# First five feature tiles of a hybrid trunk: half of the tokens projected without its shift, the shift's own projection added at evacuation

## The chip, the cores and the metric

The kernel runs on one core of a Trainium2 chip. The metric is the device time of one execution in microseconds (us); several executions of the kernel before took 1582.78 to 1583.99 us, median 1583.34. Engines are PE (TensorE, the matmuls; its weight loads are listed as PEld), DVE (VectorE), ACT (ScalarE), POOL (GpSimd) and SP, whose queue issues the transfers from device memory (DRAM) to the on-chip memory SBUF. Matmul results go to PSUM, eight banks of 2 KB for each of 128 partitions.

## The reference, cut to what matters

One inference step of a two-layer trunk over 640 tokens (128 context tokens and 512 latent ones) of 1024 features. Layer 0 runs a Conformer convolution and a bidirectional mLSTM side by side on one input projection:

```
mod = silu(cond) @ w_mod[l] + b_mod[l]             # cond: one vector for context, one for latent tokens
shift, scale, gate, ... = split(mod, 6)
h = x * rsqrt(mean(x*x, features) + eps) * g * (1 + scale) + shift
p = h @ w_in_ab
ga, gg, q, k, v, o, gates = split(p)
u = ga * sigmoid(gg)                               # then 31 taps along the tokens, layer norm, silu
gates = gates + b_gate                             # log-space scans over the tokens, once forward, once backward
```

Shift, scale and gate are one row of 1024 features for all context tokens and one for all latent tokens. Where the text below says A, it means g * (1 + scale), times the normalised x; h @ W is then the projection of the scaled x plus the projection of the shift. Layer 1 is attention; each layer is followed by a SwiGLU network. Everything is float32.

## The kernel before

The activations lie with the features on the partitions: xT is [128 partitions, 8 feature blocks k, 640 tokens]. The tokens are worked on in two halves of 320 (`HF`); in the first half the first 128 tokens are context and have their own column of the modulation (`RANGES`). Float32 accuracy comes from splitting both operands into a high and a low part and issuing three matmuls for each block k (`mm3`, L185 to L190): weight-high by H-high (L188), weight-high by H-low (L189), weight-low by H-high (L190). A feature tile for one half is 8 x 3 = 24 matmuls of 320 columns. ACT makes a high part (a copy to the rounded type), DVE or POOL the low part (source minus high part): of weights in `split_w` (L105, L108), at the start in halves (`split_half`, L586, L588), of activations in `split_to` (L464, L465).

**The first five feature tiles** of layer 0 are two tiles of convolution u0 (gg and ga), the tile of the gates, and two tiles of convolution u1. `start_norm` (L550) prepares what they need, and `proj_A(start=True)` (L413) runs them: first half of the tokens, blocks 0 to 3 of all five tiles, blocks 4 to 7 of all five tiles, then the second half tile by tile. Between the tiles it calls pieces of `start_norm` that were put into `pending` (`third`, `fourth`, `tail`, `late`). `start_norm` does, for a half:

- squares of x on ACT (L610, L613), added on DVE (L614);
- `rstd_T` (L382): sum over the partitions by two matmuls with a matrix of ones (L387, listed as four passes), root on ACT (L388) with a load of its table, reciprocal on DVE (L389), all 128x320;
- scaling of x by it, two of four tiles on DVE and two on POOL (L622).

The modulation of the whole norm comes in four pieces (which, half): which is 0 for the shift and 1 for the scale, half is features 0 to 511 or 512 to 1023. A piece takes eight row matmuls (`mod_rows`, L243), a transpose on DVE (`rows_T`, L259), four small matmuls (L250) and an add (L253, in `mod_cols`). For the first half, x is multiplied by A (L634, L636), and the shift is added as H is written (L641 on ACT for the high part, L642 on DVE for the low part), so PE's first projection matmul stands behind the pieces (1,0) and (0,0). For the second half, `modulate` (L400, L402) and `split_to` write H.

**Loads** go through SP's queue, in program order: x of the first half, eight of the modulation (L569), halves of the five weight tiles (L577) with the rest of the modulation between them, x of the second half, the other weight halves. Later modulation rows (layer 0's other pieces, blocks of 128x512) come through `mfill` (L193) and a ring of seven buffers, `mraw`; later weights through two `raw` buffers (L93).

**What comes after**: the evacuations of the conv tiles (sigmoid on ACT, L737, product on DVE, L740), of the gates (L1030, `gate_evac`); a copy of gate rows between partitions by DMA (L1089); `gate_rows` (L818): log-sigmoid on ACT (L830 to L832), scans on DVE that give M (L849, L857, L859), its split; projection of v (`v_in`), whose PSUM tiles are emptied by ACT (L1060); eight feature tiles (u2, q and k, u3, ...); a block of small matmuls on the gates (L887, L894) that ACT's copies, exponentials (L878, L900) and evacuations (L1069) release; further feature tiles. Beside all that DVE, ACT and POOL work on the 31 taps of the convolutions in the background: 21 on DVE (L756, L758), ten products on ACT (L762, L766) which POOL adds up (L767).

PSUM: tag `p1` has six buffers here, `cy` one of two banks. A scheduler fixes the order of the instructions on each engine from the program and its own model of durations; engines wait for each other by semaphores.

## Time and profile before

| | |
|---|---|
| time, median of 3 runs (lowest, highest) | 1583.34 us (1582.78, 1583.99) |
| the profiled execution: its own time | 1582.84 us |
| the profiled execution: span of the core | 1580.9 us |
| PE busy | 1520.2 us, 96% |
| DVE busy | 947.8 us, 60% |
| ACT busy | 583.7 us, 37% |
| POOL busy | 589.2 us, 37% |
| mean granted clock of PE over the span | 0.985 |

The span runs from the first to the last instruction of the profiled execution; all times below count from its start. A row of the trace with xcount over 1 stands for instructions of the same form that follow one another. What an instruction waited for stands in brackets. Busy time overlaps between engines; the chain of waits says which of it sets the end.

### The profile page before, as it was taken

The numbers are of one execution on the slowest core, as the hardware profiler recorded it, in microseconds if no ns is written. First come the engines' busy times: TensorE is split into PE (matmuls) and PEld (weight loads), VectorE is DVE, ScalarE is ACT, GpSimd is POOL, SyncE is SP. The second block draws the span as 40 slices with busy tenths as digits, with TensorE's granted clock in tenths as the row PEclk, the third lists the DMA queues.
The fourth block names the chain that finished last, engine by engine and source line by source line (L and its number), as shares of the span: only waits on it lengthen the run. The fifth ranks groups of instructions, "written<-read, shape, count | busy, mean of one in ns | idle before, by whom it ended". The sixth has DMA issues, their size and how long they took to land.

```text
span 1580.9 us, 23994 instructions
## 1 busy us (share of the span) xinstructions
PE 1520.2 (96%) x9597; PEld 1404.1 (89%) x9597; DVE 947.8 (60%) x1484; ACT 583.7 (37%) x1166; POOL 589.2 (37%) x386
## 2 busy tenths in 40 slices
PE   6898999999999999999998999999999999999998
PEld 4788988879999999999997777899998998999996
DVE  4788842647994785646768588847763423333335
ACT  3556547525222221213134437644531221212223
POOL 1479611215322112313133445524424534434241
PEclk8999999999999999999999999999999999999999
DMA  9223132442453342314352220022320321312221
GB/s 367 102 71 134 44 107 88 136 161 94 153 180 115 115 152 94 134 60 148 107 172 108 81 80 16 26 107 82 121 91 35 107 80 54 107 54 81 80 67 67
DMA packets 63684, 165.13 MB, mean 104 GB/s; under 512 B 6951, under 2 KB 13999, under 8 KB 63573
## 3 DMA queue, kind: packets, MB, share of 16 engines
q1 hardware_dynamic: 63572, 163.60, 30.1%
q8 instruction: 75, 1.23, 0.3%
q14 instruction: 37, 0.30, 0.1%
HBM read 157.45 MB, written 6.03 MB: 103 GB/s over the span
## 4 chain that ended last, share of the span: by engine, by line
PE 76%; DVE 13%; issue 4%; ACT 3%; POOL 1%; DMA 1%; SPq 0%; ACTq 0%; DVEq 0%; POOLq 0%
PE p L188 23%; PE p L189 23%; PE p L190 23%; DVE acc L220 2%; DVE t L400 1%; DVE H L465 1%; PE p L243 1%; PE p L1333 1%; DVE t L389 1%; ACT w L105 1%; DVE cy L758 1%; PE p L1353 1%; POOL t L767 1%; DVE w L108 1%; DVE acc L218 0%
## 5 line engine op out<-in xcount | busy, mean ns | idle before, releaser
L188 PE MATMUL p<-H,w 128*128 128x320 f32 x1968 | 611.5, 313 | 4.5 <-ACT h L900 1.2
L189 PE MATMUL p<-H,w 128*128 128x320 f32 x1968 | 610.8, 311 | 5.2 <-DVE H L465 5.2
L190 PE MATMUL p<-H,w 128*128 128x320 f32 x1968 | 607.7, 310 | 0.1
L108 POOL TENSOR_TENSOR w<-raw,w 128x1024 fp32r<-128x1024 f32 x124 | 316.6, 2557 | 682.2 <-ACT w L105 655.2
L188 PEld LDWEIGHTS p<-H,w 128*128 128x128 f32 x1968 | 370.4, 189 | 13.4 <-issue 3.9
L189 PEld LDWEIGHTS p<-H,w 128*128 128x128 f32 x1968 | 371.7, 189 | 11.8 <-DVE H L465 6.4
L190 PEld LDWEIGHTS p<-H,w 128*128 128x128 f32 x1968 | 370.8, 189 | 1.0 <-DVE w L588 0.5
L105 ACT ACTIVATE w<-raw 128x1024 fp32r<-128x1024 f32 x180 | 188.5, 1056 | 378.0 <-PE p L190 252.9
L220 DVE SCALAR_TENSOR_TENSOR acc<-mraw,cs,acc 128x512 f32<-128x512 f32 x196 | 175.9, 944 | 0.0
L1437 DVE TENSOR_TENSOR t<-t,p 128x320 f32<-128x320 f32 x88 | 42.6, 484 | 205.7 <-ACT t L1436 137.8
L478 DVE SCALAR_TENSOR_TENSOR h<-p,modT,h 128x128 f32<-128x128 f32 (+2 forms) x189 | 74.4, 430 | 67.6 <-PE p L190 67.5
L465 DVE TENSOR_TENSOR h<-t,h 128x320 fp32r<-128x320 f32 x88 | 93.5, 1063 | 33.0 <-ACT h L464 33.0
L188 PE MATMUL p<-h,w 128*128 128x320 f32 x352 | 108.7, 309 | 2.2 <-DVE t L1437 1.5
L1436 ACT ACTIVATE t<-p 128x320 f32<-128x320 f32 x88 | 38.3, 436 | 195.3 <-PE p L190 195.3
L189 PE MATMUL p<-h,w 128*128 128x320 f32 x352 | 108.7, 309 | 0.0
L190 PE MATMUL p<-h,w 128*128 128x320 f32 x352 | 108.3, 308 | 0.0
L108 DVE TENSOR_TENSOR w<-raw,w 128x1024 fp32r<-128x1024 f32 x56 | 77.5, 1384 | 42.4 <-ACT w L105 42.4
L471 DVE TENSOR_TENSOR t<-p,h 128x512 f32<-128x512 f32 (+1 forms) x61 | 41.4, 681 | 82.8 <-PE p L190 82.7
L472 POOL TENSOR_TENSOR h<-h,t 128x512 f32<-128x512 f32 x50 | 69.2, 1387 | 51.5 <-DVE t L471 51.4
L189 PE MATMUL p<-w,h 128*128 128x512 f32 (+1 forms) x224 | 87.5, 390 | 0.0
L190 PE MATMUL p<-w,h 128*128 128x512 f32 (+1 forms) x224 | 87.3, 390 | 0.0
L188 PE MATMUL p<-w,h 128*128 128x512 f32 (+1 forms) x224 | 87.0, 388 | 0.0
(315 smaller groups left out, 2228.0 us busy)
## 6 DMA issues: line engine op xcount, KB each, us to landing
raw<-in_wfi SPq DMA_DIRECT2D x88, 512.0 KB, 3.6
mraw<-in_wmod SPq DMA_DIRECT2D x160, 256.0 KB, 3.0
raw<-in_wfo SPq DMA_DIRECT2D x44, 512.0 KB, 3.5
raw<-in_wab SPq DMA_DIRECT2D x16, 512.0 KB, 3.5
raw<-in_wc SPq DMA_DIRECT2D x12, 512.0 KB, 3.5
h<-in_xT SPq DMA_DIRECT2D x16, 320.0 KB, 5.6
wm<-in_wmod SPq DMA_DIRECT2D x8, 512.0 KB, 7.8
h<-in_wmod SPq DMA_DIRECT2D x8, 512.0 KB, 8.2
```

What stands on the lines that cost most here:

```text
L105: self.nc.scalar.activation(hi, r, AF.Copy)
L108: e.tensor_tensor(lo, r, hi.bitcast(F32), ALU.subtract)
L188: t.matmul(out, w[0], x[0], start=first, stop=False)
L189: t.matmul(out, w[0], x[1], start=False, stop=False)
L190: t.matmul(out, w[1], x[0], start=False, stop=last)
L220: nc.vector.scalar_tensor_tensor(acc[:, c], w, s, bias if k == 0 else acc[:, c], ALU.mult, ALU.add)
L465: j = self.nc.vector.tensor_tensor(lo, src, hi.bitcast(F32), ALU.subtract)
L471: nc.vector.tensor_tensor(tmp, ps, gate, ALU.mult)
L472: (e or nc.gpsimd).tensor_tensor(x, x, tmp, ALU.add)
L478: self.nc.vector.scalar_tensor_tensor(x, ps[:, b - a * HF:e - a * HF], gate[:, k, c:c + 1], x, ALU.mult, ALU.add)
L1436: nc.scalar.activation(s[:, sl], pg, AF.Silu)
L1437: nc.vector.tensor_tensor(s[:, sl], s[:, sl], pu, ALU.mult)
```

## The change

It concerns the first five feature tiles only.

1. **First half without shift.** `no_shift` (in place of `times_A` and `plus_shift`) writes the first half's H as x*A: high part on ACT, low part on DVE by one instruction that multiplies and subtracts. The second half's H has the shift as before.
2. **The shift's projection.** H has 32 more columns; two of them take the split shift of the context and latent tokens. The second half's matmuls run over 322 columns instead of 320, so the last two columns of each tile's result are the shift's own projection. ACT copies them to SBUF (five small copies), and they are added as a bias when the first half's PSUM tile is emptied: in the sigmoid, in the product, in the gates' bias. The first half of a tile is therefore evacuated only after its second half was projected, and the tiles' order in the second half is u1, u0, gates.
3. **`rstd_P`** in place of `rstd_T` at the start: sums over the partitions by six one-column matmuls with the tokens on the partitions, root and reciprocal of 128x3 instead of 128x320, spreading by three matmuls into PSUM; scaling is all on DVE and reads that PSUM tile. The load of ACT's table is issued before it (`self.table()`).
4. **Order.** The scale pieces (1,0) and (1,1) come first, the shift pieces (0,0) and (0,1) after the first half's projection (`fifth`), the second of them through eight `mraw` buffers' turns. Loads follow: scale rows and weight halves, then x of the second half, then the shift rows. `mraw` has six buffers instead of seven. H of the first half with its shift, which v and all later tiles read, is written by `last`, under the second half's projection.
5. `start_proj` holds this loop; `proj_A` loses its `start` branch.

The diff, cut to its core (L-numbers of the printed code above are of before):

```diff
-        while self.mq and len(self.mready) < 7:
+        while self.mq and len(self.mready) < 6:
...
+        self.Hall = c.tile([P, KD, 2, TOK + 32], FR, name="H")
+        self.Hbuf = self.Hall[:, :, :, :TOK]
...
+        def dma_k(which, half):
+            for k in range(KD):
+                r = wm[which, half, k] = mraw()
+                nc.sync.dma_start(r, I["wmod"][0, 2 * which + half, k // 2][:, (k % 2) * 512:(k % 2 + 1) * 512])
...
-        def scale(a, on_pool):
-            r = self.rstd_T([sums[a][:, 0], sums[a][:, 1]], sums[a][:, 0])
+        def scale(a):
+            r = self.rstd_P([sums[a][:, 0], sums[a][:, 1]])
             sl = slice(a * HF, (a + 1) * HF)
             for i in range(4):
-                e = nc.gpsimd if i in on_pool else nc.vector
-                e.tensor_tensor(xT[i][:, :, sl], xT[i][:, :, sl], r.unsqueeze(1).to_broadcast([P, 2, HF]), ALU.mult)
+                nc.vector.tensor_tensor(xT[i][:, :, sl], xT[i][:, :, sl], r.unsqueeze(1).to_broadcast([P, 2, HF]),
+                                        ALU.mult)
...
+        def no_shift(k):
             for b, e, c in RANGES[0]:
...
+                w, A, hi = xT[k // 2][:, k % 2, b:e], m[:, 1, k, c:c + 1], H[:, k, 0, b:e]
+                nc.scalar.activation(hi, w, AF.Copy, scale=A)
+                nc.vector.scalar_tensor_tensor(H[:, k, 1, b:e], w, A, hi.bitcast(F32), ALU.mult, ALU.subtract)
         for i in range(4):
+            self.load_x(i, 0, xT[i])
+        dma(1, 0)
         for i in range(2):
             dma_w(i, 0, mraw())
+        dma(1, 1)
         for i in range(2, 5):
             dma_w(i, 0, mraw())
         rw = [self.pool.tile([P, 1024], F32, tag="raw", name="raw", bufs=2) for _ in range(2)]
         for i in range(5):
             dma_w(i, 1, rw[i // 2][:, (i % 2) * 512:(i % 2 + 1) * 512] if i < 4 else mraw())
+        for i in range(4):
+            self.load_x(i, 1, xT[i])
+        dma(0, 0)
...
+        self.table()
+        scale(0)
         mm((1, 0))
         cols(1, 0)
...
+            no_shift(k)
...
+        def second():
             mm((1, 1))
             for i in range(2, 5):
                 split_half(i, 0)
             cols(1, 1)
             for k in range(4, 8):
+                no_shift(k)
+        def third():
+            for i in range(5):
+                split_half(i, 1)
+            dma_k(0, 1)
+            for i in range(4):
+                squares(1, i)
         def fourth():
+            self.table()
+            scale(1)
+        def fifth():
+            mm((0, 0))
+            cols(0, 0)
+            mm((0, 1))
             cols(0, 1)
             for i in range(4):
                 to_H(1, i)
+            sh = m[:, 0]
+            hi, lo = (self.Hall[:, :, j, TOK:TOK + 2] for j in range(2))
+            self.split_to(hi, lo, sh)
+        def last():
+            for i in range(4):
+                to_H(0, i)
+        self.pending += [second, third, fourth, fifth, last]
...
+    def rstd_P(self, sums):
+        nc = self.nc
+        pt = self.p1()
+        blocks = ((0, 0), (P, 0), (HF - P, 2 * P - (HF - P)))
+        for j, (b, _) in enumerate(blocks):
+            for i, ss in enumerate(sums):
+                nc.tensor.matmul(pt[:, j:j + 1], ss[:, b:b + P], self.one8[:, 0:1], start=(i == 0),
+                                 stop=(i == len(sums) - 1))
+        r = self.col(8)
+        self.root = nc.scalar.activation(r[:, 0:3], pt[:, 0:3], AF.Sqrt, bias=self.eps, scale=1.0 / D).ins,
+        nc.vector.reciprocal(r[:, 4:7], r[:, 0:3])
+        pr = self.p1()[:, :HF]
+        for j, (b, o) in enumerate(blocks):
+            nc.tensor.matmul(pr[:, b + o:b + P], r[:, 4 + j:5 + j].to_broadcast([P, P]), self.ident[:, o:], start=True,
+                             stop=True)
+        return pr
+
+    def start_proj(self, H, jobs, bg):
...
+        tiles = [(i, j) for i, job in enumerate(jobs) for j in range(len(job[0]))]
+        for n, (i, j) in enumerate(tiles):
+            mm(i, j, 0, range(4))
+            self.pend((1, 4).count(n))
+        for n, (i, j) in enumerate(tiles):
+            mm(i, j, 0, range(4, KD))
+            self.pend((2, 4).count(n))
+        for n, i in enumerate((2, 0, 1)):
+            ws, evac = jobs[i]
+            for j in range(len(ws)):
+                mm(i, j, 1, range(KD))
+            if n == 0:
+                self.pend(1)
+            bias = []
+            for j in range(len(ws)):
+                b = self.col(2)
+                nc.scalar.activation(b, outs[i, j, 1][:, HF:], AF.Copy)
+                bias.append(b)
+            evac(slice(0, HF), *[outs[i, j, 0] for j in range(len(ws))], bias=bias)
+            evac(slice(HF, TOK), *[outs[i, j, 1][:, :HF] for j in range(len(ws))])
+            self.tick(bg[0] / 6, bg[1] / 6)
+            self.wdone(len(ws))
```

The order of the instructions on three queues, before and with the change (line numbers of each kernel's own code; `p` and `cy` are PSUM tiles, `H` the activations, `w` weights, `wm`, `h` and `mraw` buffers of modulation rows, `cs` the conditioning vectors, `fsel` a selection matrix, `xcount` at the end as in the profile).

PE, from its start to the first projection matmul; before:

```order
L669 MATMUL p_147<-ident 128x128 x18
L387 MATMUL p_176<-t,one_76 128x320 x2
L243 MATMUL p_185<-wm,cs 32x512 x8
L250 MATMUL p_196<-t,fsel 32x8 x4
L243 MATMUL p_211<-wm,cs 32x512 x8
L250 MATMUL p_231<-t,fsel 32x8 x4
L669 MATMUL p_237<-ident,t 128x128 x4
L188 MATMUL p_272<-H,w 128x320
```

and with the change:

```order
L650 MATMUL p_141<-ident 128x128 x18
L711 MATMUL p_172<-one_76,t 128x1 x6
L718 MATMUL p_182<-ident,col 128x128 x2
L718 MATMUL p_182<-ident,col 128x64
L243 MATMUL p_190<-wm,cs 32x512 x8
L250 MATMUL p_201<-t,fsel 32x8 x4
L188 MATMUL p_247<-H,w 128x320
```

One modulation piece (L243, L250) instead of two stands ahead of the first projection matmul, and the norm's matmuls have one column in place of 320.

PE, where the first half's projection ends (in `cy`) and the second half's begins; before:

```order
L190 MATMUL cy<-H,w 128x320
L188 MATMUL p_515<-H,w 128x320
L188 MATMUL p_540<-H,w 128x320
L188 MATMUL p_583<-H,w 128x320
L188 MATMUL p_614<-H,w 128x320
L188 MATMUL p_639<-H,w 128x320
L189 MATMUL p_515<-H,w 128x320
```

and with the change:

```order
L190 MATMUL cy<-H,w 128x320
L243 MATMUL p_467<-h,cs 32x512 x8
L250 MATMUL p_478<-t,fsel 32x8 x4
L243 MATMUL p_484<-mraw,cs 32x512 x8
L250 MATMUL p_495<-t,fsel 32x8 x4
L188 MATMUL p_519<-H,w 128x322
L188 MATMUL p_544<-H,w 128x322
L188 MATMUL p_619<-H,w 128x322
L189 MATMUL p_519<-H,w 128x322
```

Both shift pieces, sixteen row matmuls and eight small ones, have moved from ahead of the first half and from within it to this place.

SP's queue around the copy of the gate rows (`h<-h`); before:

```order
L197 DMA mraw<-in_wmod 128x512 x5
L93 DMA raw<-in_wv 128x1024 x2
L197 DMA mraw<-in_wmod 128x512
L93 DMA raw<-in_wv 128x1024 x2
L93 DMA raw<-in_wab 128x1024
L1089 DMA h<-h 36x640
L197 DMA mraw<-in_wmod 128x512 x4
L93 DMA raw<-in_wab 128x1024 x3
```

and with the change:

```order
L93 DMA raw<-in_wv 128x1024 x2
L566 DMA mraw<-in_wmod 128x512
L93 DMA raw<-in_wv 128x1024
L566 DMA mraw<-in_wmod 128x512 x2
L197 DMA mraw<-in_wmod 128x512 x6
L93 DMA raw<-in_wv 128x1024
L93 DMA raw<-in_wab 128x1024 x3
L197 DMA mraw<-in_wmod 128x512 x4
L1142 DMA h<-h 36x640
```

The copy of the gate rows (L1142 with the change) now has three weight loads and four modulation loads directly ahead of it; before it had one weight load there, and those others behind it.

## Rows read from the trace of the kernel before

**Rows 1.** The page's first part: busy time, share of the span and number of instructions of each engine over the whole span.

```profile
PE 1520.2 (96%) x9597; PEld 1404.1 (89%) x9597; DVE 947.8 (60%) x1484; ACT 583.7 (37%) x1166; POOL 589.2 (37%) x386
```

**Rows 2.** Timeline of all engines from 0 to 62 us, the rows of the chain up to the first projection matmul (L188) and one later transpose. Columns: start in us, duration in us (of all instructions of a row together), engine, line, operation, output<-input, tile sizes, xcount; in brackets the idle time of the engine before it and what ended it.

```profile
9.78 0.82 DVE L614 TENSOR_TENSOR t<-t 128x640 f32<-128x640 f32 x1 [0.33 <-ACT t L613]
...
10.66 2.50 PE L387 MATMUL p<-t,one 128*128 128x320 f32 x4 [5.15 <-DVE t L614]
...
13.23 1.28 ACT L388 ACT_TABLE_LOAD   x1 [3.48 <-PE p L387]
...
17.73 3.90 DVE L622 TENSOR_TENSOR h<-h,t 128x640 f32<-128x640 f32 x2
...
17.86 0.25 PE L250 MATMUL p<-t,fsel 128*32 128x8 f32 x8 [1.79 <-DVE t L259]
...
21.56 0.15 DVE L253 TENSOR_TENSOR modT<-p,vecs 128x8 f32<-128x8 f32 x1
...
25.06 0.56 PE L188 MATMUL p<-H,w 128*128 128x320 f32 x2 [0.66 <-ACT H L641]
...
33.83 0.72 DVE L259 STREAM_TRANSPOSE t<-p 128x512 f32<-128x512 f32 x1 [4.14 <-PE p L243]
```

**Rows 3.** PE's own timeline from 48 to 82 us: the second half's norm (L387), the first matmul of the second half's projection after the first half's last, the row after which the second half's projection has no more gap, and its last matmul. Columns as in rows 2.

```profile
48.63 2.47 PE L387 MATMUL p<-t,one 128*128 128x320 f32 x4 [4.55 <-DVE t L614]
...
61.47 0.85 PE L188 MATMUL p<-H,w 128*128 128x320 f32 x4 [0.46 <-ACT H L464]
...
64.45 0.41 PE L189 MATMUL p<-H,w 128*128 128x320 f32 x1 [0.61 <-DVE H L465]
...
81.26 0.31 PE L190 MATMUL p<-H,w 128*128 128x320 f32 x1
```

**Rows 4.** Groups of DVE instructions of one line, operation and tile size between 72 and 195 us, and one such group of the page, over the whole span. Columns: line, engine, operation, output<-input, tile sizes, xcount | busy us, mean ns of one | idle us before them and what ended most of it.

```profile
L758 DVE SCALAR_TENSOR_TENSOR cy<-t,vecs,cy 128x655 f32<-128x655 f32 x80 | 72.2, 903 | 2.5
...
L220 DVE SCALAR_TENSOR_TENSOR acc<-mraw,cs,acc 128x512 f32<-128x512 f32 x196 | 175.9, 944 | 0.0
```

**Rows 5.** A window of the trace, 46.0 to 52.8 us: its length, then busy us and (x) instructions of PE, PE's weight loads, DVE, ACT and POOL, then PE's granted clock as a share of full speed, the DMA share and GB/s.

```profile
46.00:52.80 6.80, 4.07 (x10) 2.91 (x10) 6.75 (x13) 4.76 (x11) 4.02 (x3) 0.50 0.01 2
```

**Rows 6.** The DMA view of 0 to 90 us: GB/s in 40 equal slices of 2.25 us.

```profile
GB/s 32 255 294 352 410 424 415 417 419 417 411 418 424 399 363 383 401 367 276 15 0 4 4 7 350 229 4 0 233 0 0 0 9 310 193 2 0 245 267 188
```

**Rows 7.** The page's part on DMA issues, over the whole span: output<-input, queue, kind, xcount, KB each, median us from issue to landing.

```profile
mraw<-in_wmod SPq DMA_DIRECT2D x160, 256.0 KB, 3.0
...
raw<-in_wab SPq DMA_DIRECT2D x16, 512.0 KB, 3.5
```

**Rows 8.** From the gate projection to the scans and past v: rows of the timelines of ACT, SP's queue, DVE and PE between 57 and 111 us, in order of time. Columns as in rows 2; an SP row is the issue of a DMA.

```profile
57.26 0.64 ACT L402 ACTIVATE h<-h,modT 128x320 f32<-128x320 f32 x1
...
74.86 0.53 ACT L1030 ACTIVATE h<-p,vecs 100x320 f32<-100x320 f32 x1
...
75.42 0.88 SPq L1089 DMA_DIRECT2D h<-h  x1
...
79.53 0.74 ACT L830 ACTIVATE h<-h 36x640 f32<-36x640 f32 x1 [1.80 <-DMA h<-h]
...
82.50 0.50 PE L188 MATMUL p<-w,H 128*128 128x512 f32 x1
...
86.50 0.82 DVE L834 TENSOR_TENSOR h<-h 36x640 f32<-36x640 f32 x1 [2.05 <-ACT h L832]
...
108.46 0.74 ACT L464 ACTIVATE h<-h 36x640 fp32r<-36x640 f32 x1 [9.78 <-DVE h L859]
...
109.20 0.58 ACT L1060 ACTIVATE h<-p 128x512 f32<-128x512 f32 x1
...
110.27 0.31 PE L188 MATMUL p<-H,w 128*128 128x320 f32 x1
```

**Rows 9.** PE's own timeline from 138 to 156 us, the gate block: the last matmul of the eight feature tiles, the block's small matmuls (L894), a modulation group (L243) and the first matmul of the next feature tile; then, of the waits of PE between 149 and 232 us, the longest that isn't in these rows (us in total, times, longest). Columns of the others as in rows 2.

```profile
139.02 0.31 PE L190 MATMUL p<-H,w 128*128 128x320 f32 x1
...
140.58 0.76 PE L894 MATMUL p<-ident,h 36*128 36x36 f32 x8 [0.67 <-ACT h L1069]
141.28 1.06 PE L243 MATMUL p<-mraw,cs 128*32 128x512 f32 x8
145.96 0.64 PE L894 MATMUL p<-ident,h 36*128 36x36 f32 x4 [3.62 <-ACT h L1069]
147.00 0.64 PE L894 MATMUL p<-ident,h 36*128 36x36 f32 x4 [0.40 <-ACT decb L889]
148.81 0.63 PE L188 MATMUL p<-H,w 128*128 128x320 f32 x1 [1.17 <-ACT h L900]
...
PE p L799 <- DVE t L986: 0.6, 1, 0.6
```

**Rows 10.** POOL and ACT around the gate block: one row of each engine's timeline (columns as in rows 2), POOL's two large groups between 72 and 195 us, and ACT's half of the weight split from the page (columns as in rows 4).

```profile
118.32 2.40 POOL L108 TENSOR_TENSOR w<-raw,w 128x1024 fp32r<-128x1024 f32 x1
...
144.75 0.84 ACT L766 ACTIVATE t<-t,vecs 128x655 f32<-128x655 f32 x1 [2.94 <-POOL t L767]
...
L767 POOL TENSOR_TENSOR t<-t 128x655 f32<-128x655 f32 x36 | 59.6, 1658 | 15.4 <-ACT t L766 14.0
...
L108 POOL TENSOR_TENSOR w<-raw,w 128x1024 fp32r<-128x1024 f32 x12 | 28.8, 2401 | 12.5 <-ACT w L105 12.5
...
L105 ACT ACTIVATE w<-raw 128x1024 fp32r<-128x1024 f32 x180 | 188.5, 1056 | 378.0 <-PE p L190 252.9
```

More of the change, by code (lines that the diff above doesn't have):

```diff
@@ L410, in H_tile, with proj_A @@
         return self.Hbuf
-    def proj_A(self, H, *jobs, bg=(), start=False):
-        early = bool(self.pending) and not start
+    def proj_A(self, H, *jobs, bg=()):
+        early = bool(self.pending)
         for a in range(2):
@@ L580, in mraw @@
         def mraw():
-            return self.pool.tile([P, 512], F32, tag="mraw", name="mraw", bufs=7)
+            return self.pool.tile([P, 512], F32, tag="mraw", name="mraw", bufs=6)
         def split_half(i, b):
@@ L671, in start_norm @@
-        warm(self.ident, 18)
-        for i in range(4):
-            squares(0, i, nc.vector)
-        if 0:
-            self.table()
-        scale(0, (2, 3))
+        for i in range(4):
+            self.load_x(i, 1, xT[i])
+        dma(0, 0)
+        ps = self.p1()
+        for _ in range(18):
+            nc.tensor.transpose(ps[:, :P], self.ident, self.ident)
+        for i in range(4):
+            squares(0, i)
+        self.table()
+        scale(0)
         mm((1, 0))
         cols(1, 0)
-        for k in range(4):
-            times_A(k)
@@ L681, in start_norm @@
-        mm((0, 0))
         for i in range(5):
@@ new lines, in last @@
+        def last():
+            for i in range(4):
+                to_H(0, i)
[16 more added lines that the diff above has]
+        return pr
@@ L1027, in ab_layer, with gate_evac @@
         Rt = self.ht()
[L1029 to L1030 removed]
+        def gate_evac(sl, p, bias=None):
+            if bias:
+                b = self.col(2)
+                nc.vector.tensor_scalar(b, bias[0], self.vec("bgate"), None, ALU.add)
+                for c, (s, e) in enumerate(((0, P), (P, HF))):
+                    nc.scalar.activation(Rt[:100, s:e], p[:100, s:e], AF.Identity, bias=b[:100, c:c + 1])
+            else:
+                nc.scalar.activation(Rt[:100, sl], p[:100], AF.Identity, bias=self.vec("bgate")[:100])
         def conv(j, *bg):
```

126 lines of the change are left out of this document (44 added, 82 removed).

## The prediction

> **What bounds the kernel now.** The page's first part comes first: TensorE (PE) is busy for 96% of the span [rows 1]. Busy time of the other engines is therefore worth nothing by itself; a change pays where it removes an idle stretch of PE that nothing later swallows. Then the merged timeline of the first 35 us [rows 2]: the reader is to see one chain, in which each step is released by the one before it, from the last add of the squares at 9.78 to the first projection matmul at 25.06. Then PE's own timeline [rows 3]: it stands idle 4.55 us until the second half's row norm can start at 48.63, waits 0.46 and 0.61 us more for H, and the second half's projection then runs from 64.45 to 81.4 without a gap, 115 matmuls 0.147 us apart. What follows, v, eight feature tiles and one more idle stretch between 139 and 149, comes in steps 4 and 5.
>
> **The sum** is made against the profiled execution (1582.84 us, span 1580.9; the median of the runs is 1583.34, 0.5 us above it). Times are from the span's start.
>
> *Step 1, to the first matmul.* The sum of squares ends at 10.60. Now follow 2.50 of PE, 1.28 of table load, the root and the reciprocal, so that scaling starts only at 17.73, and 3.90 of it on DVE (POOL does the other two tiles beside it), to 21.6; the scale columns, the scaled product and the shift columns lead to 25.06 [rows 2]. The change puts six one-column matmuls (twelve passes) in L387's place. No row has this form: eight passes with a quarter of the weight columns take 0.25 us (L250), which makes 1.5 us from below, and L387's 2.50 is the bound from above; I take 2.2, nearer L387 since that has the same weight columns. The table load moves ahead and hides under them. Root and reciprocal of three columns I put at 0.25 and 0.2, as small operations go (L253 takes 0.15). Spreading the result over the partitions takes half of L387's passes over the same columns, 1.25. Scaling is now four tiles on DVE with one operand in PSUM. The row of the old scaling says 1.95 each with POOL at work; L614, with two SBUF operands and POOL idle, 0.82 [rows 2]; L758, with one operand in PSUM, 0.90 while POOL adds tap products most of the time [rows 4]. I take 0.85, as L758 is nearest in form: 3.4. The Trainium skill (SBUF — State Buffer, Who interferes with whom) says that a DVE instruction with at most one SBUF input, outside the two-port modes, does not contend with GpSimd. By that rule the step costs 3.4, by the old row 7.8; the trace agrees with the rule in L758's 0.90. So 10.6 + 2.2 + 0.25 + 0.2 + 1.25 + 3.4 = 17.9; transpose (0.72), L250 (0.25) and two column operations with their waits make 1.6; the first piece of H and its wait 0.6: **20.1 instead of 25.06**. The shift no longer stands in between.
>
> *Step 2, the first half.* PE has 120 matmuls, 17.6; eight modulation matmuls in three pieces, about 3.8; the small one-column ones of the second norm and of the second scale half 1.7; spreading the second norm 0.7; and some matmuls at half clock after the idle, as now between 46 and 52.8, where the granted clock was 0.50 [rows 5], 0.7. The loads are no limit: DMA moves about 0.41 MB/us from 9 us on [rows 6]; in the new order the product half (1,1) is in by about 19, the second half of x by 27, the shift half (0,0) by 32. The half ends at **44.6 instead of 61.0**, which is 61.47 less the 0.46 us of idle before it [rows 3].
>
> *Step 3, the shift, now between the halves.* (0,0): 2.1 of matmuls, 0.72 of transpose, 0.25: 47.7. (0,1) comes in eight pieces through six buffers, so its last two loads are issued only when PE has used the first two, at 48.3; 3.0 to land [rows 7] and 0.5 for the second behind the first: 51.8; then 0.3 of matmuls, 0.72, 0.25, 0.15 and 0.2 of waits: 53.4. On ACT two modulations (0.64 each) stand ahead of the shift's split [rows 8], and PE's first low-part matmul waits for DVE's half of that: 55.8. The kernel of before has this wait hidden under projection, and waits for squares and for H instead. Then 120 matmuls, 17.7 with two more columns each, and 1.1 for eight at half clock: the five tiles end at **74.6 instead of 81.4, 6.8 us earlier**. Bounds: 71 (no half clock, the norm's matmuls at the low bound, loads landing 2 us sooner) and 79 (scaling at the old row's price).
>
> *Step 4, what is behind it.* PE goes on to both groups of the second layer's modulation (2.1) and to v (27.8, from 82.50 to 110.27) and is through at 104.5. It then needs a PSUM bank: of tag p1's six, five hold v tiles and one the modulation rows. ACT empties the first v tile at 109.20, right behind its half of the split of M, the end of the scans, at 108.46 [rows 8]. So the gate chain decides. In the change the gate tile is the last of five, at 74.6, and the tile before it ends at 71.1. From there ACT has two tap starts and four tap products ahead of the gate's second half (0.84 each), a weight half, and copies and evacuations of some 2.2: 8.3 with the weight half's 1.06, so 79.4, against 74.86 + 0.53 = 75.4 now. The copy of the gate rows takes 4.1 again (75.42 to 79.53): 83.5. ACT's three steps and two table loads after it take 4.9: 88.4. From there M takes DVE 108.46 - 86.50 = 22.0 now; in the new order two tap adds fewer (0.90) lie in it: 20.1. M comes at **108.5, as now**. PE is thus held from 104.5 to 110.3, where now it goes on at 110.27: all of the 6.8 us is given back here, and 1.1 us more with the clock at its lower level after the idle.
>
> *Step 5, where some of it returns.* The eight tiles take 28.9: 140.3. The gate block takes 9.8 us now: 5.9 idle (0.67 + 3.62 + 0.40 + 1.17), 1.06 for a modulation group that the change moves ahead, 2.8 of work [rows 9]. The idle is ACT's: L1069 stands behind a tap product that waited 2.94 for POOL, and POOL has had no pause since 118.32 [rows 10]. In the new order twelve instead of nine tap products stand ahead of ACT's exponential of the gates, so POOL has three adds (1.66 each) less to do in this stretch. Bounds: none of the wait left, 143.1; all of it, 149.0. I take 144.5, 1.4 us of wait, since weight loads that follow one another through two raw buffers still hold ACT: **4.3 us ahead of 148.81**. After this PE's longest wait up to 232 is 0.6 (L799), and nothing on its order changes.
>
> *At no cost:* the second modulation and split of the first half (some 3 us of DVE and 4 of ACT) run under the second half's projection and are needed by v; without that cover they cost as much as they take. Six instead of seven modulation buffers still hold 6 x 2 x 0.94 = 11 us of L220's work against 3.0 to land [rows 4, 7]. The bias copies are five small ACT steps under matmuls. Sum: 1583.34 - 4.3 = **1579.0**.
>
> **Rivals.** (B) All 6.8 us stay, 1576.5: if the v tiles are emptied without waiting for M, or M comes 5 us earlier. For it: POOL and ACT have less in their way; against it: the v evacuations stand behind M in ACT's order. (C) The head start is spent twice, M where it is now and the gate block's wait unchanged: 1583.5, no difference. For it: DVE works through a close queue of taps and scans up to M, whatever comes before. (D) Slower, by one place: SP's queue has the copy of the gate rows behind three weight loads and four modulation loads, where now one weight load stands there. A weight load's turn is 3.5 to land, 1.06 and 2.4 for the two parts of its split, 7.0 in all [rows 7, 10]. I have all of them issued by 78. If one more turn comes first, M slips to 115 and PE with it: 4.3 - 6.8 = 2.5 us slower, 1585.8. It decides from a copy issued later than 83.7.
>
> **How the numbers follow.** My case 0.50 (own range 1577 to 1582), B 0.18, C 0.21, D 0.11. A difference below 0.2% (3.2 us) is about what a measurement of this kernel cannot tell from none. Of my case 0.36 lies above that: faster 0.36 + 0.18 = 0.54; same 0.14 + 0.21 = 0.35; slower 0.11. The range reaches from B with the low bound of step 3 (2.5 us more of B) to a part of D: 1574 to 1584.5.
>
> **What would show it.** First projection matmul at 20 (19 to 22); first half done at 43 to 47; second half from 54 to 58, and an idle of 5 to 8 us ahead of it that follows the last two shift loads; five tiles done at 72 to 78; PE idle at about 104 to 110, released by an evacuation that follows M; M at 107 to 111; the first tile after the gate block at 143 to 147. A gate-row copy after 84, or no idle at 104, would make it wrong.

## The result and the profile after

| | before | after |
|---|---|---|
| median of six runs (lowest, highest) | 1583.37 us (1582.76, 1583.99) | 1590.46 us (1586.68, 1592.68) |
| ratio, 95% interval | | 1.0043 [1.0031, 1.0054] |
| profiled execution: own time, span | 1582.84, 1580.9 us | 1590.37, 1588.5 us |
| mean granted clock | 0.985 | 0.982 |

The change makes the kernel 7.1 us (0.4%) slower; the forecast was 1579.0. Ratios here are of undisturbed runs alone and need not be the quotient of the medians.

The page's first part after, against [rows 1]:

```profile
PE 1528.4 (96%) x9621; PEld 1409.8 (89%) x9621; DVE 949.0 (60%) x1493; ACT 587.1 (37%) x1179; POOL 583.1 (37%) x383
```

PE's idle time has not grown (1588.5 - 1528.4 = 60.1 us, before 60.7). Its busy time has, by 8.2. By the mean granted clock at most some 5 us of that (an estimate: 1.8% of 1588.5 against 1.5% of 1580.9) come from matmuls at the lower clock. That looks like a verdict on the clock; experiment e3 shows that it isn't.

The start, from the timelines of DVE and PE after (columns as in [rows 2]); it answers to [rows 2, 3]:

```profile
10.38 2.72 PE L711 MATMUL p<-one,t 128*128 128x1 f32 x12 [4.56 <-DVE t L610]
13.67 1.54 PE L718 MATMUL p<-ident,col 128*128 128x128 f32 x6 [0.56 <-DVE col L715]
15.24 3.02 DVE L617 TENSOR_TENSOR h<-h,p 128x640 f32<-128x640 f32 x4 [1.63 <-PE p L718]
21.18 0.90 PE L188 MATMUL p<-H,w 128*128 128x320 f32 x2 [1.27 <-ACT H L629]
48.12 0.31 PE L190 MATMUL cy<-H,w 128*128 128x320 f32 x1
48.36 1.92 PE L243 MATMUL p<-h,cs 128*32 128x512 f32 x16
55.06 2.00 PE L243 MATMUL p<-mraw,cs 128*32 128x512 f32 x4 [1.80 <-DMA mraw<-in_wmod]
60.73 1.02 PE L188 MATMUL p<-H,w 128*128 128x322 f32 x3 [2.61 <-ACT H L454]
82.11 0.31 PE L189 MATMUL p<-H,w 128*128 128x322 f32 x1
82.49 1.07 PE L243 MATMUL p<-mraw,cs 128*32 128x512 f32 x8
83.48 0.50 PE L188 MATMUL p<-w,H 128*128 128x512 f32 x1
```

The first projection matmul comes 3.9 us earlier and the first half ends near 48.4 instead of 61, but the shift and its waits fill 48.4 to 60.7, and the five tiles end at 82.4, which is 1.0 later than before. Windows of the same execution (columns as in [rows 5]) show part of why:

```profile
10.00:20.00 10.00, 8.13 (x42) 4.79 (x42) 4.26 (x8) 2.35 (x5) 2.80 (x8) 0.50 1.03 415
20.00:27.00 7.00, 5.82 (x20) 2.50 (x21) 6.05 (x13) 6.62 (x16) 2.84 (x2) 0.51 1.06 398
60.70:68.00 7.30, 6.27 (x23) 5.87 (x24) 5.02 (x12) 4.13 (x8) 0.00 (x0) 0.53 0.00 0
121.50:125.00 3.50, 3.49 (x13) 3.49 (x14) 3.46 (x5) 3.28 (x5) 2.09 (x3) 0.50 0.38 116
```

The granted clock is at its lower level through the start, and again in the two stretches that follow PE's idle before 60.7 and before 121.5. From 26 to 27 and from 63 to 67 the projection matmuls start 0.27 us apart, where they otherwise start 0.147 apart. In the first window the lower clock does not show: e3, whose granted clock was 1.00 there, has the same 2.72, 1.54 and 3.64 us for the twelve passes, the spreading and the first modulation piece as the kernel after.

From the gates to the gate block: timelines of ACT, SP's queue, DVE and PE after, by start; they answer to [rows 8, 9]:

```profile
83.09 1.56 ACT L813 ACTIVATE t<-t,vecs 128x655 f32<-128x655 f32 x2
84.55 0.92 ACT L809 ACTIVATE t<-t,vecs 128x655 f32<-128x655 f32 x1
85.38 0.83 ACT L813 ACTIVATE t<-t,vecs 128x655 f32<-128x655 f32 x1
85.63 2.14 SPq L197 DMA_DIRECT2D mraw<-in_wmod  x4
86.16 0.51 ACT L1083 ACTIVATE h<-p,vecs 100x320 f32<-100x320 f32 x1
86.57 1.05 ACT L105 ACTIVATE w<-raw 128x1024 fp32r<-128x1024 f32 x1
87.52 0.83 ACT L813 ACTIVATE t<-t,vecs 128x655 f32<-128x655 f32 x1
88.25 0.66 ACT L1081 ACTIVATE h<-p,col 100x128 f32<-100x128 f32 x2
88.94 0.89 SPq L1142 DMA_DIRECT2D h<-h  x1
92.37 0.74 ACT L877 ACTIVATE h<-h 36x640 f32<-36x640 f32 x1 [1.65 <-DMA h<-h]
98.07 9.35 DVE L805 SCALAR_TENSOR_TENSOR cy<-t,vecs,cy 128x655 f32<-128x655 f32 x10
107.33 8.43 DVE L896 TENSOR_TENSOR_SCAN h<-h 4x128 f32<-4x128 f32 x10
120.14 0.74 ACT L454 ACTIVATE h<-h 36x640 fp32r<-36x640 f32 x1 [9.95 <-DVE h L906]
120.89 0.58 ACT L1113 ACTIVATE h<-p 128x512 f32<-128x512 f32 x1
121.51 0.63 PE L188 MATMUL p<-H,w 128*128 128x320 f32 x1 [8.93 <-ACT h L1113]
153.43 0.43 PE L941 MATMUL p<-ident,h 36*128 36x36 f32 x4 [0.23 <-ACT decb L936]
155.24 0.42 PE L188 MATMUL p<-H,w 128*128 128x320 f32 x1 [1.37 <-ACT h L947]
```

PE is through with the gate tile at 82.4, but ACT's order puts tap work (L809, L813) and a weight half ahead of its emptying (L1083, L1081), so the copy of the gate rows is issued at 88.94, 13.5 us later than in [rows 8]. M follows at 120.14 instead of 108.46, the v evacuation follows M, and PE stands 8.93 us behind it. It resumes 11.2 us later than before (121.51 against 110.27), and the eight tiles, which now begin at the lower clock, take 1.3 us more; the gate block gives 6.1 back (idle 1.6 instead of 5.9, 1.1 for a modulation group that now stands at 111.52, 0.8 of the rest). 11.2 + 1.3 - 6.1 = 6.4, which is 155.24 against 148.81. The remaining 1.2 us of the span's 7.6 are lost later and not assigned.

### The profile page after: what moved, and what is told of

Read it like the earlier page. It is cut to its first block, busy times and chain, and to the rows that moved or that the text cites. A ratio compares the mean times of both kernels' runs of the same rounds, so it can differ in the third digit from the quotient of the medians.

```text
span 1588.5 us, 24065 instructions
## 1 busy us (share of the span) xinstructions
PE 1528.4 (96%) x9621; PEld 1409.8 (89%) x9621; DVE 949.0 (60%) x1493; ACT 587.1 (37%) x1179; POOL 583.1 (37%) x383
## 3 DMA queue, kind: packets, MB, share of 16 engines
q8 instruction: 76, 1.25, 0.3%
## 4 chain that ended last, share of the span: by engine, by line
PE 80%; DVE 13%; ACT 3%; issue 2%; DMA 1%; POOL 1%; SPq 0%; DVEq 0%; ACTq 0%; POOLq 0%
PE p L188 24%; PE p L189 23%; PE p L190 23%; DVE acc L220 3%; PE p L243 2%; DVE H L455 1%; DVE t L400 1%; PE p L1386 1%; DVE cy L805 1%; ACT w L105 1%; PE p L1406 1%; DVE t L389 1%; DVE w L108 1%; DVE h L896 1%; DVE acc L218 0%
## 5 line engine op out<-in xcount | busy, mean ns | idle before, releaser
L188 PE MATMUL p<-H,w 128*128 128x320 f32 (+1 forms) x1968 | 611.2, 313 | 14.9 <-ACT h L1113 8.9
L189 PE MATMUL p<-H,w 128*128 128x320 f32 (+1 forms) x1968 | 612.0, 311 | 5.6 <-DVE H L455 5.6
L190 PE MATMUL p<-H,w 128*128 128x320 f32 (+1 forms) x1968 | 609.6, 310 | 0.0
L188 PEld LDWEIGHTS p<-H,w 128*128 128x128 f32 x1968 | 371.6, 190 | 26.1 <-ACT h L1113 9.8
L105 ACT ACTIVATE w<-raw 128x1024 fp32r<-128x1024 f32 x180 | 188.6, 1056 | 374.0 <-PE p L190 250.2
L188 PE MATMUL p<-h,w 128*128 128x320 f32 x352 | 109.5, 311 | 1.6 <-DVE t L1490 1.1
L188 PE MATMUL p<-w,h 128*128 128x512 f32 (+1 forms) x224 | 87.2, 389 | 0.0
```

The costliest lines, as they stand in the source:

```text
L105: self.nc.scalar.activation(hi, r, AF.Copy)
L188: t.matmul(out, w[0], x[0], start=first, stop=False)
L189: t.matmul(out, w[0], x[1], start=False, stop=False)
L190: t.matmul(out, w[1], x[0], start=False, stop=last)
```

## The experiments

Each kernel is the changed one or the one before with one edit. "Copy" is the issue of the gate rows' copy, M the start of ACT's half of its split, the next column PE's wait behind v, and "tile" the first feature tile's matmul behind the gate block, all in us of the profiled execution. In e2, where the split starts on POOL, M is the end of the last scan. The kernel before ran again beside the experiments (medians 1583.4 to 1583.9), and each ratio is against those runs; the first row has the runs beside the kernel after. A profile is one execution: in the seven kernels that share the changed start (after, e1, e2, e3, e9, e12, e13) the first half alone ends between 46.1 and 48.4. A difference of 2 us between two rows may be such chance; the intervals rest on all runs.

| kernel | median | ratio [95%] | copy | M | M - copy | wait | tile |
|---|---|---|---|---|---|---|---|
| before | 1583.4 | | 75.42 | 108.46 | 33.0 | 0.5 | 148.81 |
| after | 1590.5 | 1.0043 [1.0031, 1.0054] | 88.94 | 120.14 | 31.2 | 8.9 | 155.24 |
| e1 | 1590.1 | 1.0041 [1.0028, 1.0055] | 71.12 | 103.71 | 32.6 | 6.1 | 153.72 |
| e2 | 1601.3 | 1.0110 [1.0091, 1.0129] | 86.31 | 113.5 | 27.2 | 11.9 | 158.39 |
| e3 | 1595.2 | 1.0074 [1.0052, 1.0095] | 85.33 | 116.06 | 30.7 | 9.0 | 151.87 |
| e4 | 1586.3 | 1.0016 [1.0007, 1.0026] | 84.08 | 117.01 | 32.9 | 7.4 | 152.59 |
| e5 | 1586.2 | 1.0015 [1.0006, 1.0024] | 77.89 | 109.61 | 31.7 | 2.6 | 149.59 |
| e6 | 1588.8 | 1.0026 [1.0013, 1.0039] | 83.23 | 115.79 | 32.6 | 9.1 | 151.65 |
| e7 | 1581.7 | 0.9986 [0.9975, 0.9996] | 73.66 | 108.56 | 34.9 | 2.5 | 148.79 |
| e8 | 1589.0 | 1.0026 [1.0012, 1.0041] | 88.23 | 120.57 | 32.3 | 9.4 | 155.83 |
| e9 | 1590.3 | 1.0044 [1.0029, 1.0058] | 87.70 | 118.02 | 30.3 | 8.2 | 153.88 |
| e10 | 1582.5 | 0.9996 [0.9986, 1.0005] | 76.25 | 107.47 | 31.2 | none | 149.12 |
| e11 | 1586.5 | 1.0021 [1.0011, 1.0030] | 68.90 | 103.81 | 34.9 | 6.6 | 153.22 |
| e12 | 1589.8 | 1.0035 [1.0023, 1.0047] | 89.74 | 118.76 | 29.0 | 8.7 | 153.90 |
| e13 | 1599.1 | 1.0098 [1.0076, 1.0121] | 88.37 | 120.42 | 32.1 | 9.8 | 162.79 |

**e1: the changed kernel, gate tile first in the second half.**

```diff
-        for n, i in enumerate((2, 0, 1)):
+        for n, i in enumerate((1, 2, 0)):
```

> The changed kernel with the gate tile as the first of the second half's tiles (order gates, u1, u0) and nothing else. Theory (gate chain): the copy of the gate rows is issued at about 71 instead of 88.9, M comes at 100 to 106 instead of 120.1, PE's wait of 8.9 us after v is gone, part of the gain is lost again at the gate block: 1583 to 1587. Rival (the loss is the clock at its lower level, and the later half start): the five tiles still end at 82 and the clock still falls after the shift's wait, so M is not what counts: 1588 to 1591.

M comes at 103.71 and PE goes on behind v without a wait, yet it then stands still for 6.1 us, up to 123.52, in e1's timelines of ACT and PE:

```profile
112.83 0.21 ACT L925 ACTIVATE sm<-sm 36x5 f32<-36x5 f32 x1 [3.72 <-DVE sm L924]
122.05 0.84 ACT L813 ACTIVATE t<-t,vecs 128x655 f32<-128x655 f32 x1 [1.35 <-POOL t L814]
122.89 0.58 ACT L1113 ACTIVATE h<-p 128x512 f32<-128x512 f32 x1
123.52 0.64 PE L188 MATMUL p<-H,w 128*128 128x320 f32 x1 [6.12 <-ACT h L1113]
```

On ACT the third v tile's evacuation stands behind an exponential (L925) that waited 3.72 us for DVE and behind tap products that waited 3.2 us for POOL (1.04, 0.84 and 1.35). A late M is enough to hold PE, but an early M does not free it, because other work now stands ahead of the evacuation in ACT's order. The time is that of the changed kernel and within the rival's range.

**e2: M's high part on POOL**, to take M's split out of ACT's queue.

```diff
-        self.split_to(Mh, Ml, M)
+        nc.gpsimd.tensor_copy(Mh, M)
+        nc.vector.tensor_tensor(Ml, M, Mh.bitcast(F32), ALU.subtract)
```

> The changed kernel with the high part of M's split on POOL instead of ACT; the gate chain stays as late as it is. Theory (PE's wait after v is ACT's order: the emptying of v's PSUM tiles stands behind M's split on ACT): the v tiles are emptied soon after they are done, PE goes on at about 112.6 without a wait of more than 1 us, M still comes at 118 to 121; time 1583 to 1587. Rival (PE waits for something else as well, buffers or weights): a wait of 5 us or more stays at that place under another name, time within 1.5 us of the changed kernel's.

M came 27.2 after the copy, the shortest of all, and the first v tiles were emptied at 107.4, ahead of it. But PE then waited 11.9 us up to 128.93 for an evacuation of a conv tile (L780). On ACT that stands behind the exponential L925, which waited 15.4 us for DVE, and DVE spent 9.2 of these on one copy:

```profile
114.46 9.21 DVE L918 COPY sm<-h 4x5 f32<-4x5 f32 x1
```

The same copy takes 0.16 us in the changed kernel; here POOL was at work beside it from 113.58 to 123.6. So the wait moved to another place, as the rival had it, and the kernel got slower than either expectation. It says that the orders on ACT and DVE matter, and no more.

**e3: filler transposes on PE while it waits**, to keep the clock up.

```diff
+                if b == (0, 1) and k == 6:
+                    ps = self.p1()
+                    for _ in range(10):
+                        nc.tensor.transpose(ps[:, :P], self.ident, self.ident)
...
+            ps = self.p1()
+            for _ in range(12):
+                nc.tensor.transpose(ps[:, :P], self.rows_tr[:, :P], self.ident)
```

> The changed kernel with 22 idle transposes on PE in the waits for the shift: ten ahead of the last two modulation matmuls, twelve ahead of the second half's first matmul. Theory: the clock is granted in full at 61 to 68, the five tiles end at about 79.5 instead of 82.4, the gate chain and the whole kernel come 2.9 us earlier: 1586.5 to 1588.5. Rival (transposes that do no work don't keep the clock, or they delay the matmuls behind them): 1590 to 1593.

Windows of e3, to be read beside those of after:

```profile
10.00:20.00 10.00, 7.70 (x41) 4.36 (x41) 4.24 (x8) 2.03 (x6) 2.81 (x8) 1.00 1.02 409
58.80:66.00 7.20, 5.85 (x38) 5.59 (x39) 5.03 (x12) 4.14 (x8) 0.00 (x0) 1.00 0.01 2
205.00:217.00 12.00, 10.22 (x58) 7.72 (x57) 9.21 (x25) 6.17 (x19) 0.00 (x0) 0.86 0.14 49
```

v starts at 79.36 instead of 83.48. Of these 4.1 us, 1.8 are there before the first filler (the first half ends at 46.54 instead of 48.36) and have nothing to do with the edit; 2.2 come in the second half's projection, with the clock at its upper level, so the clock explains that much of the missing head start. PE then waits 9.0 us behind M all the same, and the tile comes 3.4 earlier. Between 202 and 223 a lead of 2.2 us turns into 1.2 of delay: PE waits for DVE in the layer norm of the convolution, and part of the stretch runs at the lower clock. Another 3 us are lost between 277 and 304, where the clock is low again (0.57 up to 285). The kernel is slower still, and slower than either expectation, at a mean clock of 0.987 against 0.982.

**e4: the kernel before, with the gate tile last.**

```diff
-            for i, (ws, evac) in enumerate(jobs):
+            for i in (0, 2, 1) if start and a else range(len(jobs)):
+                ws, evac = jobs[i]
```

> The kernel before with the gate tile as the last of the second half's five tiles (order u0, u1, gates), nothing else changed. Theory (gate chain): gates come 7 us later, M at about 115.5 instead of 108.5, PE waits some 6 us after v: 1587 to 1590. Rival (the gate chain has that much slack): within 1 us of the kernel before, 1583 to 1584.5.

The copy comes 8.7 us later, M 8.6 later, PE waits 7.4 and the tile comes 3.8 later; the time grows by 0.16%, 2.4 us in the medians. The place of the gate tile alone, without shift or norm, makes the kernel slower. SP's queue has a part in it, in e4's timelines of ACT and SP:

```profile
82.03 0.51 ACT L1031 ACTIVATE h<-p,vecs 100x320 f32<-100x320 f32 x1
82.29 1.75 SPq L197 DMA_DIRECT2D mraw<-in_wmod  x4
84.08 0.87 SPq L1090 DMA_DIRECT2D h<-h  x1
```

ACT has emptied the gate tile at 82.54, but the copy is issued 1.5 us after that, directly behind four modulation loads.

**e5 and e6: the changed kernel, u0 first, the gate tile in the middle (e5) or last (e6).** `cy` goes to u0's first half.

```diff
-                if a == 0 and i == 2:
+                if a == 0 and i == 0:
...
-        for n, i in enumerate((2, 0, 1)):
+        for n, i in enumerate((0, 1, 2)):
```

(e6: `(0, 2, 1)`.)

> The changed kernel with the second half's tiles in the order u0, gates, u1 (as in the kernel before), and u0's first half instead of u1's in the two-bank PSUM tile that the taps' sum needs. Two theories by now. Taps: since a conv tile is emptied only after its second half, DVE's and POOL's taps start at 81 instead of 72 and DVE, which has no pause from 82 to 155, carries that on to M and to the gate block. Gates: the gate tile's last place alone. Here the taps start at about 73 and the gate rows are copied at about 79: by the taps theory M comes at 108 to 113, PE's wait after v is under 3 us, the first tile after the gate block comes at 147 to 151, time 1582 to 1586; if neither counts, 1589 to 1592.

> As the kernel with the order u0, gates, u1, but in the order u0, u1, gates: the taps start at about 73, the gates stay last. Taps theory: M at 113 to 117, with fewer taps left when the scans begin, time 1584 to 1588, nearer to the order u0, gates, u1 than to the changed kernel. Gates theory: as the changed kernel, M at 119 to 121, 1589 to 1592.

The two differ in the place of the gate tile alone: copy 5.3, M 6.2 and the wait 6.5 us apart, the times 2.6 (the intervals of the two overlap). PE of e5 at the gate block:

```profile
141.36 0.44 PE L941 MATMUL p<-ident,h 36*128 36x36 f32 x4 [0.65 <-ACT h L1121]
146.74 0.64 PE L941 MATMUL p<-ident,h 36*128 36x36 f32 x4 [3.95 <-ACT h L1122]
147.78 0.64 PE L941 MATMUL p<-ident,h 36*128 36x36 f32 x4 [0.40 <-ACT decb L936]
149.59 0.64 PE L188 MATMUL p<-H,w 128*128 128x320 f32 x1 [1.17 <-ACT h L947]
```

With M in time again, the idle of [rows 9] is back in full, 0.65 + 3.95 + 0.40 + 1.17 = 6.2. What e5 still loses beyond the tile's 0.8 us (2.65 in the medians) is open.

**e7: the kernel before with the new norm alone** (`rstd_P` as in the change, all scaling on DVE, the early table load).

```diff
-            r = self.rstd_T([sums[a][:, 0], sums[a][:, 1]], sums[a][:, 0])
+            r = self.rstd_P([sums[a][:, 0], sums[a][:, 1]])
...
-                e = nc.gpsimd if i in on_pool else nc.vector
-                e.tensor_tensor(xT[i][:, :, sl], xT[i][:, :, sl], r.unsqueeze(1).to_broadcast([P, 2, HF]), ALU.mult)
+                nc.vector.tensor_tensor(xT[i][:, :, sl], xT[i][:, :, sl], r.unsqueeze(1).to_broadcast([P, 2, HF]), ALU.mult)
...
-        if 0:
-            self.table()
+        self.table()
```

> The kernel before with the changed norm alone (one-column sums, 128x3 root and reciprocal, spreading into PSUM, scaling all on DVE), in both halves. The first projection matmul comes at 21 to 22.5 instead of 25.06 and the second half's gap at 48 shrinks, so that the five tiles end 3 to 6 us earlier, and the taps and gates with them. Taps theory: DVE starts earlier by as much, M and the gate block follow, 1579 to 1581.5. Rival (a head start at v is swallowed at the gate block in any case): 1582.5 to 1584.5.

PE's timeline of e7, behind v and at the gate block:

```profile
109.92 0.41 PE L188 MATMUL p<-H,w 128*128 128x320 f32 x1 [2.46 <-ACT h L1077]
145.94 0.64 PE L911 MATMUL p<-ident,h 36*128 36x36 f32 x4 [3.95 <-ACT h L1086]
148.79 0.63 PE L188 MATMUL p<-H,w 128*128 128x320 f32 x1 [1.17 <-ACT h L917]
```

v starts 2.9 us earlier (79.65), and all of it is gone at 148.79: 2.5 in a wait behind M, the rest at the gate block. Up to the gate block a head start on PE alone is worth nothing here. The kernel is all the same 1.9 us faster than before in the medians, between its two expectations; where that is won was not taken apart.

**e8: the kernel before, in which the first halves are emptied only after the second half's tile, in the order u1, u0, gates.**

```diff
-            for i, (ws, evac) in enumerate(jobs):
+            for i in (2, 0, 1) if start and a else range(len(jobs)):
+                ws, evac = jobs[i]
...
+                if start and a == 0:
+                    late[i] = [outs[i, j] for j in range(len(ws))]
+                    continue
+                if start:
+                    evac(slice(0, HF), *late[i])
```

> The kernel before with one part of the change alone: the first half of each of the five tiles is emptied only after its second half was projected, in the order u1, u0, gates; shift, norm and loads as before. Taps theory: the taps start at 80 to 82 instead of 72, M comes at 118 to 121, PE waits 7 to 10 us after v, time 1588 to 1592, which is the whole loss of the changed kernel. Gates theory: no slower than the kernel before with the gates last, 1585 to 1587.5.

Copy 88.23, M 120.57, wait 9.4, tile 155.83: with neither the new norm nor the moved shift, the profile of after is there from the copy to the gate block. In the medians it costs 5.4 of the 7.1 us. Of the copy's 13.5 us, 8.7 thus go with the gate tile's place (e4) and 4.2 with the emptying left for the end, of which up to 1.5 may be chance, since e8's five tiles end that much later than e4's (82.6 against 81.1). The remaining 0.7 is not assigned.

**e9 and e10: fewer taps on DVE**, in the changed kernel and in the one before. Six of the 21 taps of u0 and of u1 each are left out, so the kernels compute something else.

```diff
-            else:
+            elif j > 1 or i not in (1, 3, 5, 7, 9, 11):
```

> The changed kernel without six of DVE's 21 taps of u0 and of u1 each (left out of the result), 10.8 us less work for DVE before the gate block. Taps theory (DVE carries the late start on): M comes 5 us earlier, at 114 to 116, PE's wait after v falls to 2 to 5 us, the first tile after the gate block comes at 148 to 152 instead of 155.2, time 1583 to 1587. Rival (DVE's work is not what M and the gate block wait for): 1588.5 to 1591.

> The kernel before without the same twelve taps, as the measure for the changed kernel without them. Taps theory: M at 103 instead of 108.5 frees nothing on PE, which is busy with v until 110; at the gate block ACT and POOL still hold it; 1580 to 1583.5, so that the changed kernel's distance shrinks from 7 to 2 to 5 us. Rival: both kernels move alike and the distance stays at 6 to 8.

M - copy is 30.3 and 31.2, against 31.2 and 33.0 with all taps, and the distance between the two kernels stays as well (7.7 us). DVE's load alone was my first theory for M, and it falls. The ten scans, in the source view (line, engine, operation, count: shortest/median/longest in ns, first and last start), after and then in e9:

```profile
L896 DVE TENSOR_TENSOR_SCAN h<-h x10: 386/402/2561, 107.3 to 115.4; 4x128 f32<-4x128 f32 x10
```

```profile
L896 DVE TENSOR_TENSOR_SCAN h<-h x10: 386/1752/2464, 101.3 to 113.3; 4x128 f32<-4x128 f32 x10
```

In e9 they begin 6 us sooner and end 2 us sooner. DVE waits 1.0 us for POOL (L882) ahead of them, and they take 12.3 us together instead of 8.4: most of what the taps gave free, the scans took beside POOL.

**e11: e7 with the gate tile first** in the second half.

```diff
-            for i, (ws, evac) in enumerate(jobs):
+            for i in (1, 0, 2) if start and a else range(len(jobs)):
+                ws, evac = jobs[i]
```

> The kernel before with the changed norm, and the gate tile as the first of the second half's tiles. With the norm alone PE waited 2.5 us after v for M's split. Here the gate rows are copied 7 us earlier, at about 67, M comes at 101 to 105 and that wait is gone, but u0's taps start 3.5 us later, at about 74. If M decides: 1578.5 to 1581. If the start of the taps decides: 1582.5 to 1585.

As in e1: M at 103.81, no wait behind v, then 6.6 us up to 122.34 for the third v tile's evacuation. At 1586.5 it is slower than either expectation, and 4.8 us slower than e7 in the medians.

**e12 and e13: less work on POOL**, in the changed kernel: five of POOL's nine tap adds of u0 and of u1 each left out (e12), the four zeroings of gate rows on ACT (e13).

```diff
-                    nc.gpsimd.tensor_tensor(z, z, q, ALU.add)
+                    if j > 1 or i not in (2, 4, 6, 8, 10):
+                        nc.gpsimd.tensor_tensor(z, z, q, ALU.add)
```

```diff
-            nc.gpsimd.tensor_scalar(v, Iv, 0.0, None, ALU.mult)
+            nc.scalar.activation(v, Iv, AF.Copy, scale=0.0)
```

> The changed kernel without five of POOL's nine tap adds of u0 and of u1 each (left out of the result; ACT's products and DVE's taps stay). With six of DVE's taps fewer nothing was gained: the scans then began 6 us earlier and took 12.3 us instead of 8.4, one scan for each instruction of POOL, as long as POOL had work. POOL theory: POOL's unbroken work ahead of M ends 6 to 9 us earlier than 113.5, the ten scans take 4 to 6 us, M comes at 110 to 114, PE's wait after v is 0 to 3 us, the first tile after the gate block comes at 147 to 152; time 1582 to 1587. Rival (M waits for DVE's own taps or for ACT): M stays at 117 to 121, 1588.5 to 1591.

> The changed kernel with the four zeroings of gate rows (7.6 us of POOL) on ACT, nothing left out. In this order POOL has two more tap adds ahead of M instead, so that its work ahead of M shrinks by about 4 us. POOL theory: M comes 3 to 5 us earlier, at 115 to 117, 1586.5 to 1589. Rival: M as in the changed kernel or later (ACT has 3 us more to do), 1589.5 to 1592.

29.0 and 32.1: POOL's load alone does not set it either. In e12 six taps instead of ten stand ahead of the scans, which take 7.5 us instead of 8.4, but two copies of 4x3 behind them take 1.35 and 1.42 us, beside POOL, instead of 0.16 each. In e13 the scans take 11.5 us beside POOL's adds and M stays; the tile comes 7.5 us later, with 6.4 us of idle at the gate block instead of 1.6.

**What holds over all of them.** In 14 of 15 kernels M comes 29 to 35 us after the copy, and where M is late the tile behind the gate block follows it by 35 to 36 us (after, e3, e4, e6, e8, e9, e12). Where M is in time the tile comes no sooner than 148.8 to 149.6 (before, e5, e7, e10). e1, e2, e11 and e13 are held elsewhere, as told. What the 31.2 us of the changed kernel consist of, its rows show: 3.4 until the copy has landed, 4.9 of ACT's steps, 0.8 of DVE (L881), 9.3 for ten taps that stand ahead of the scans in DVE's order, 8.4 for the ten scans and 4.3 for the rest. Why the sum changes so little is not shown: work taken from DVE alone or from POOL alone moved M - copy by 2.2 us at most, and taking it from both at once was not tried. What sets the floor at the gate block is open too.

## Why the prediction was wrong

**Bound and steps 1 to 3.** Step 1 came out within its bounds: 21.18 for 20.1 (19 to 22). L711's 2.72 lies above the upper bound of 2.50, L718's 1.54 above 1.25; the scaling took 3.02 us for four tiles (L617), with POOL at work up to 17.4, against 3.4 in the forecast and 7.8 by L622's row. The rule of the Trainium skill that the forecast weighed there (SBUF — State Buffer, Who interferes with whom) agrees with these 3.02. Steps 2 and 3 were mis-sized: 27.1 us for 24.5 (half-clock matmuls from 21 to 27, where I had put 0.7 us for all of them), 12.4 for 11.2 in the shift's stretch, 21.7 for 18.8 in the projection behind it (0.53 granted up to 68). Of these 21.7, 2.0 pass before the first low-part matmul at 62.75, where the forecast had the border: DVE's order has six modulations (L400, 1.89 us) ahead of the shift's low part. With step 1's 1.1 that is 7.8: tiles done at 82.4 for 74.6, outside the bounds 71 to 79. The head start of 6.8 us did not exist. That alone did not make the kernel slower: e3 had v 4.1 us earlier than the changed kernel and gained nothing, and e7 had 2.9 over the kernel before and lost all of it by the gate block.

**The step that failed is step 4, and it turned the sign:** "M comes at 108.5, as now". It came at 120.14. Of the 11.6 us, 7.8 are steps 1 to 3; 1.7 are ACT's stretch ahead of the copy (88.94 for 79.4), in which three weight halves stand (L105, at 79.17, 81.30 and 86.57) where the forecast has one; the copy was 0.7 faster (88.94 to 92.37); ACT's three steps took their 4.9; and from there M took 22.8 for 20.1. The last difference is the ten scans, which the forecast left as they are before:

```profile
98.39 5.70 DVE L849 TENSOR_TENSOR_SCAN h<-h 4x128 f32<-4x128 f32 x10
```

They took 8.43 instead, with POOL at work until 113.5, where in the kernel before it stops at 101.2. I had counted ACT's queue, but I set the gate tile's place at the end and the late emptying against a head start into which only 1.8 us of half clock had gone. e8 shows the price of these two without anything else of the change: 5.4 us. The copy after 84 that "would make it wrong" is what came.

**Step 5 and rival C.** Where M is in time, nothing returns at the gate block: e5 and e7 have its wait unchanged. That is rival C's mechanism, and it should have stood above the forecast. In the changed kernel the block's idle did shrink, to 1.6 where I had 1.4, but that was luck: PE came to it 11 us later.

**Rival D** had the direction and the condition, a copy later than 83.7, but the wrong place and a small price. In the changed kernel SP's queue was not the last to hold the copy: its four loads were issued by 87.8, and the copy 0.03 us after L1081's end at 88.91. ACT's order held it, and the cost is +6.4 at the gate block, where the rival had +2.5. But the margin is 1.2 us only: with a faster ACT the copy would still have stood behind those loads, and in e4 it did, for 1.5 us.

**Rival B** is out: v's evacuations stood behind M, as the argument against it said. Its other condition, an M some 5 us earlier, was nearly met in e1 and e11 (103.7 and 103.8 against 108.46), and there the next wait took the gain.

## What to carry to other kernels

Before moving a tile within a stage that PE bounds, follow its result through the in-order queue that empties it, to the chain that next stops PE: here one small copy was issued 13.5 us later, and PE stood still for 8.9 us behind what follows from it. A chance to start PE earlier is worth trying first by itself, at its smallest (e7), since the part of a change that pays can hide behind a part that costs. A term that takes matmuls behind an idle at full clock is a bound and not an estimate.

## What the runs showed of the hardware

- **Scans beside POOL.** A scan of 4x128 with its inputs in SBUF takes 0.38 to 0.41 us in e7, where POOL stands idle beside all ten (below, in the source view, columns as in e9), and up to 2.56 in the changed kernel. In e9 their median is 1.75 us, about the 1.66 of one of POOL's tap adds [rows 10], which ran beside them. The Trainium skill (SBUF — State Buffer, Who interferes with whom) says that a DVE instruction with two SBUF inputs contends with a GpSimd instruction that reads SBUF; these numbers agree.

```profile
L866 DVE TENSOR_TENSOR_SCAN h<-h x10: 384/387/414, 100.8 to 103.8; 4x128 f32<-4x128 f32 x10
```

- **The same instructions at two clocks.** Between 10 and 20 us after and e3 have the same program on PE, and the granted clock was 0.50 in the one execution and 1.00 in the other. The twelve passes, the spreading and the first modulation piece took the same 2.72, 1.54 and 3.64 us in both, so in this stretch the granted clock does not show in the durations.
- **Fillers keep the clock.** With 22 transposes in PE's waits the clock was 1.00 in the first 7.2 us of the second half's projection; in the eight other kernels with the moved shift it was 0.53 to 0.59 there, once 0.76. It fell again behind waits at 205 to 217 and at 277 to 285.
